# Differential attention: the mix of the two softmaxes on GpSimd alone

## The chip, the cores and the metric

One core of a Trainium2 chip runs the kernel. The metric is the device time of one execution in microseconds. The engines are TensorE (PE in the profile; its weight loads are PEld), VectorE (DVE), ScalarE (ACT), GpSimd (POOL) and SyncE (SP), which issues the DMAs.

## The reference, cut to what matters

Two transformer layers on 2048 tokens of width 1024. The first layer attends in three ways at once: stick-breaking attention (6 heads), differential attention (6 heads), and attention over a memory (4 heads). The change touches the second of these. Each of its heads has two components, each with a softmax of its own over the keys up to the query, and the second softmax is subtracted, with a factor, before the product with the values:

```python
def one_block(bi):
    qi = lax.dynamic_slice_in_dim(q, bi * BLOCK, BLOCK, axis=1)
    s = jnp.einsum('bqhcd,bkhcd->bhcqk', qi, k, ...) * scale
    ...
    p = jax.nn.softmax(jnp.where(causal, s, NEG_BIG), axis=-1)
    a = p[:, :, 0] - lam * p[:, :, 1]
    return jnp.einsum('bhqk,bkhd->bqhd', a.astype(v.dtype), v)
```

An rms norm over each head's 64 features follows, then a gate, the output projection, a layer norm, and the second layer.

## The kernel before, in words

The kernel runs in stages: the projections of the first layer, the stick-breaking attention (to about 1120 us of the span), the differential attention (to about 1740 us), the join of the two layers, and the second layer. Only the differential attention is of concern here; it is the function `differential`.

Its work is cut into 24 units. A unit is a pair of heads (p = 0, 1, 2) and two blocks of 128 queries that together see 17 blocks of keys: a high block of queries with n keys (9 to 16 blocks) and a low block with the rest (8 to 1 blocks). So each row tile is 17 x 128 = 2176 columns wide, with the high block's keys first and the low block's behind them. A unit has four row tiles: x and y, the two components, for each of its two heads.

A unit goes through three stages, each a step behind the one before. While unit s+2 has its scores made, unit s+1 is mixed and unit s multiplied with the values.

- Scores (`diff_scores`): TensorE writes a chunk of up to 512 scores into one of three PSUM banks (`psz`). VectorE moves it to the row tile, negated and scaled, and keeps its minimum (L725), with the mask on the diagonal (L727); L731 joins minima. The bank is free when VectorE is done. ScalarE then takes the exponentials in place, with sums.
- Mix (`diff_mix`): VectorE makes a column of factors per head from the sums: a reciprocal (L762) and a product with minus lambda and the first component's sum (L766). One factor is for the high block and one for the low block. Then x becomes x + factor * y. The softmaxes are not normalised here: the rms norm takes the common factor out.
- Values (`diff_values`): TensorE transposes blocks of x into PSUM (`pstp`), ScalarE copies them to SBUF, and TensorE multiplies with the values. The low block's chunks come first, then the high block's. When four units have filled a chunk of 512 queries, `diff_norm` follows (L849 and L851 are its two GpSimd instructions).

A step has four beats. In a beat the scores of one row tile, the mix's steps for that beat, and chunks of the values are interleaved. Also interleaved is a filler: a share of the output projection (`psmm<-wo,mp`), whose input is split in two parts by ScalarE and GpSimd (L901), and whose result is added up on VectorE (L912).

In this stage the order on TensorE and ScalarE is that in which the program is written. The order on VectorE and GpSimd is chosen by a planner, which simulates the program with its own estimates when it is built. Nine row tiles are there; a unit takes four, y is free again after the mix and x after its transposes.

How the mix is shared before: with nlo the number of the low block's key blocks, `a` is 128 * max(0, 5 - nlo) columns. GpSimd takes columns a to n of a head: it multiplies y by the factor, which is repeated along the row as the second tensor of a two-tensor multiply (L771), and adds the product to x (L772). VectorE takes the low block's columns, in pieces of at most 1024, and columns 0 to a, each as one instruction that multiplies and adds (L778). So VectorE does 5 to 8 of the 17 blocks. Its first piece of a head comes at once with GpSimd's part; the others come a beat or more later.

Of the kernel before, what the change touches and what calls it, by code (L numbers as in the profile page):

```python
# [12 lines left out]
ALU = mybir.AluOpType  # L13
AX = mybir.AxisListType

S = 2048
D = 1024
P = 128
# [16 lines left out]
VBLOCKS = 5  # L35
MIX = 1024
# [9 lines left out]
class Pinned:  # L46
    """An engine whose instructions stay in the order in which they are written."""
# [18 lines left out]
class Net:  # L66
# [15 lines left out]
    @contextmanager  # L82
    def phase(self, bufs, banks, side="left"):
        """Pools for one phase; SBUF slots and PSUM banks by tag."""
        with ExitStack() as ctx:
            layer = {k: (n, ctx.enter_context(self.tc.tile_pool(name=self.nm("p" + k), bufs=1, side=side, reuse_waits="tile")))
                     for k, n in bufs.items()}
            if banks:
                ps = ctx.enter_context(self.tc.tile_pool(name=self.nm("pp"), bufs=1, space=bass.MemoryType.PSUM, reuse_waits="tile"))
                layer.update({"ps" + k: (n, ps) for k, n in banks.items()})  # L90
            self.layers.append(layer)
            yield
            self.layers.remove(layer)
# [20 lines left out]
    def turn(self, key, pattern):  # L114
        """The next letter of a repeated pattern: which engine takes this one."""
        k = self.turns.get(key, 0)
        self.turns[key] = k + 1
        return pattern[k % len(pattern)]
# [8 lines left out]
    def consts(self):  # L127
# [5 lines left out]
        # nothing, then what is after the query (a column further on: at it or after it)  # L133
# [12 lines left out]
        # -lambda on every partition  # L146
# [26 lines left out]
    def rope_tables(self, k, sink):  # L173
        """cos and sin of the positions' angles, in chunks of 512: sink(chunk, cos, sin)."""
        nc = self.nc
        for t in range(NT):
            posi = self.t("c2", I32)
            self.dma(posi, self.i["pos"][t * TC:(t + 1) * TC].partition_broadcast(P))
            ang = self.t("c2")
            nc.vector.tensor_copy(ang, posi)  # L180
            nc.vector.tensor_scalar_mul(ang, ang, self.freq[:, k:k + 1])
            n = self.t("c2")
            nc.vector.tensor_scalar(n, ang, 1.0 / TWO_PI, MAGIC, ALU.mult, ALU.add)
            nc.vector.tensor_scalar_add(n, n, -MAGIC)
            for c in (C1, C2, C3):
                nc.vector.scalar_tensor_tensor(ang, n, -c, ang, ALU.mult, ALU.add)
            nc.vector.tensor_scalar(ang, ang, math.pi, -math.pi, ALU.min, ALU.max)
            nc.scalar.activation(n, ang, AF.Abs)
            sink(t, n, ang)
            yield  # L190

# [1 line left out]
    def wtile(self, src):  # L193
        """A [P, 8, 128] tile of weights, as two parts."""
        w, (fill,) = self.wtile_steps(src, 1, self.nc.gpsimd)
        fill()
        return w
# [21 lines left out]
    def load_x(self, between):  # L219
        """x transposed, [tc][half] -> (hi, lo) of [P, 4, 512]."""  # L220
# [22 lines left out]
    def proj_t(self, w, t):  # L243
        """[128 features, 512 tokens] of chunk t."""
        return self.proj_side([w], t)[0]

    def proj_side(self, ws, t):
        """The same for several tiles of weights side by side."""
# [8 lines left out]
    def spill_parts(self, ps, dst, t, scale=None):  # L257
        """ps (times a power of two) in two parts to dst [2, P, S]."""
# [112 lines left out]
    def rope_all(self):  # L371
        """Both layers' tables to DRAM, a chunk of one at each next()."""
# [13 lines left out]
    def vtile(self, g):  # L386
        """Weights of 256 columns of the two attentions' values, as two parts of each half."""
# [9 lines left out]
    def values(self, g, ws, side):  # L397
        """256 columns of the two attentions' values, token by token."""
# [19 lines left out]
    def dup_parts(self, hi, lo, src, hh):  # L418
        """Half hh of src's partitions, its two parts in both halves of hi and lo."""
# [13 lines left out]
    def memkv(self, W, mem, keep):  # L433
        """Memory keys of each pair of heads and all values, a weight tile at each next()."""
# [35 lines left out]
    def tblocks(self, blocks, pattern="AV"):  # L470
        """Up to four [P, P] blocks transposed, in SBUF."""
# [8 lines left out]
    def softmax_pair(self, z, e, n0, sink=False):  # L480
        """z [P, 2, 256] -> e, normalised; columns from n0 on; the first is the sink's."""
# [13 lines left out]
    def mem_scores(self, qs, qcol, mk):  # L495
        """One block of queries, heads 2f and 2f+1 over the memory."""
# [20 lines left out]
    def load_qstack(self, src, t):  # L517
        """[P = two copies of 64, 2 heads, 2 parts, 512]."""
# [9 lines left out]
    def load_sb(self, p):  # L528
        """A pair of heads' keys and values and the last chunk's queries."""
# [69 lines left out]
    def differential(self):  # L599
        """Differential attention in three stages, each a unit (two blocks of queries, 17 blocks of  # L600
        keys together, of two heads) behind the one before: scores and exponentials; the mix of the
        two softmaxes; the product with the values. Between them go some feature tiles' share of
        the output projection."""
# [10 lines left out]
        def mixed(a, b):  # L614
            """Two lists evenly mixed, each in its order."""
# [58 lines left out]
    def load_dq(self, p, k, h):  # L674
        """Queries of a half of each of the two chunks: units j = 2h and 2h + 1."""
# [7 lines left out]
    def diff_parts(self, unit):  # L683
        """Of the two blocks of queries: their number, the chunk's, the place in it, the keys, the
        first column in a row."""
# [4 lines left out]
    def diff_scores(self, unit, rows):  # L690
        """For each head and component the steps of its scores, and those of the exponentials."""
# [56 lines left out]
    def diff_mix(self, unit, rows):  # L748
        """Steps by beat."""
        p, k, j = unit  # L750
        parts = self.diff_parts(unit)
        nlo = parts[1][3] // P
        a = P * max(0, VBLOCKS - nlo)
        cf = {}

        def take(steps):
            for f in steps:
                f()
# [9 lines left out]
        def mix(hh):  # L768
            x, y = rows[unit][0][2 * hh][0], rows[unit][0][2 * hh + 1][0]
            n = parts[0][3]  # L770
            self.nc.gpsimd.tensor_mul(y[:, a:n], y[:, a:n], cf[hh][:, :1].to_broadcast([P, n - a]))  # L771
            self.nc.gpsimd.tensor_add(x[:, a:n], x[:, a:n], y[:, a:n])  # L772
            pieces = [(c, min(c + MIX, 17 * P), 1) for c in range(n, 17 * P, MIX)]
            if a:
                pieces.append((0, a, 0))
            for lo, hi, w in pieces:
                def piece(lo=lo, hi=hi, w=w):
                    self.nc.vector.scalar_tensor_tensor(x[:, lo:hi], y[:, lo:hi], cf[hh][:, w:w + 1], x[:, lo:hi], ALU.mult, ALU.add)  # L778
                late[hh].append(piece)
            late[hh].pop(0)()  # L780

        late = [], []
        i0, f0, m0, l0 = lambda: inverse(0), lambda: factor(0), lambda: mix(0), lambda: take(late[0])
        i1, f1, m1, l1 = lambda: inverse(1), lambda: factor(1), lambda: mix(1), lambda: take(late[1])
        return [[i0, f0, m0], [l0, i1, f1, m1], [], [l1]]
# [36 lines left out]
    def diff_norm(self, p, t, s0, pv, tail):  # L822
        """rms norm over each head's 64, scaled by the first sum; the rest of its steps to tail."""
# [42 lines left out]
    def filler(self):  # L866
        """alpha x and the share of the output projection of the feature tiles known before the
        differential attention; lists of steps."""
# [60 lines left out]
    def memory(self, mk, mv):  # L929
        """The first layer's attention over the memory, a block at each next(), to go  # L930
        between other projections."""
# [52 lines left out]
    def out_proj(self, w, msrc, spans, res, alpha, lng, lnb, tbs, ahead):  # L984
        """A block of the output projection and its layer norm at each next()."""
# [50 lines left out]
    def join(self, tail):  # L1036
        """The rest of the first layer's output projection, its norm, x of the second layer
        transposed in two parts, and its first gates; the steps in tail go between."""
# [60 lines left out]
    def qstack_head(self, qs, src, hh, eng):  # L1099
        """The two parts of head hh's queries (half of src's partitions), one on top of the other."""  # L1100
# [4 lines left out]
    def qstack_from(self, src, eng):  # L1105
        """[P = two parts of 64, 2 heads, 512] of a tile of two heads' queries (in SBUF)."""
# [22 lines left out]
    def swa_scores(self, qb, head, qs, qcol, ks):  # L1129
        """Heads head and head+1 over a block of keys and the one before; the first  # L1130
        column of that one is out of every query's window and takes the sink."""
# [37 lines left out]
    def gates(self, W, dst, om=None, m1=None, order=None, ws=None):  # L1169
        """silu of the gates to dst; times what has been attended to m1 where that is known."""  # L1170
# [27 lines left out]
    def layer2_kv(self):  # L1198
        """Keys in two parts and values of each group, to DRAM."""
# [35 lines left out]
    def layer2(self):  # L1235
        """The projections of queries go in quarters between the blocks of the attention, whose
        three stages lie a block or two apart."""
# [238 lines left out]
```

## Time and profile before

| | |
|---|---|
| time, median of 3 runs | 2660.3 us (2658.35 to 2661.22) |
| profiled execution, span from the first to the last instruction | 2665.1 us |
| mean granted TensorE clock in it | 0.969 |
| busy in the span: PE, DVE, ACT, POOL | 94%, 62%, 47%, 45% |
| GpSimd's multiply (L771) and add (L772), 48 each | 132.9 and 163.3 us |
| VectorE's multiply-and-add (L778), 72 | 153.2 us |

The profiled execution has no time on record beside its span; the median of the runs is 4.8 us below that span. Durations below are those of the profiled execution. In a row of groups, the columns are the line, engine, operation, output and inputs with their shapes, the count, then busy time and mean duration in ns, then the idle time of the engine just before with what ended it. A row of the timeline begins with the start and the duration in us; brackets hold the idle time before the instruction and what released it. A row of waits gives who waited for whom, the total in us, how often, and the longest.

### The profile page before, as it was taken

How to read it: one execution, taken by the hardware profiler on the slowest of the kernel's cores; microseconds unless marked ns; L12 is line 12 of the kernel's file. 1: busy time of each engine (PE TensorE's matmuls, PEld its weight loads, DVE VectorE, ACT ScalarE, POOL GpSimd, SP SyncE). 2: the span in 40 equal slices, each digit the busy share in tenths (PEclk: the TensorE clock that was granted, in tenths of full speed). 3: DMA queues.
4: the chain of work that ended last, by engine and by line, in shares of the span. 5: the costliest groups of instructions: out<-in, count | busy, mean ns of one | idle time of the engine just before them, and what ended most of it. 6: DMA issues, size and time to landing. Idle time of an engine off the chain costs nothing. (4 is left out here: it accounts for less than half of the span.)

```text
span 2665.1 us, 42634 instructions
## 1 busy us (share of the span) xinstructions
PE 2503.5 (94%) x15564; PEld 1964.7 (74%) x15564; DVE 1656.7 (62%) x3672; ACT 1264.2 (47%) x2653; POOL 1189.9 (45%) x848
## 2 busy tenths in 40 slices
PE   9899999999989999968877988999999999999998
PEld 7788998888757777646655666678788777777887
DVE  5732223421379999888889878788321667677554
ACT  4532222221167777555665765744121677776200
POOL 1301004730056666465646746764541555535333
PEclk9999999999989999989988988999999999999999
DMA  7643223321842331442523422265332555532541
GB/s 273 212 146 125 70 88 105 137 103 52 203 104 70 82 71 34 99 116 73 127 78 95 108 76 74 70 215 173 88 101 75 162 154 162 152 96 99 194 147 67
DMA packets 199250, 311.60 MB, mean 117 GB/s; under 512 B 17921, under 2 KB 97281, under 8 KB 198529
## 3 DMA queue, kind: packets, MB, share of 16 engines
q1 hardware_dynamic: 198464, 307.83, 39.3%
q8 instruction: 123, 2.02, 0.3%
q10 hardware_dynamic: 576, 1.05, 0.1%
q14 instruction: 87, 0.70, 0.1%
HBM read 204.74 MB, written 104.07 MB: 116 GB/s over the span
## 5 line engine op out<-in xcount | busy, mean ns | idle before, releaser
L56 PE MATMUL psmm<-big,w 128*128 128x512 f32 x1680 | 415.4, 395 | 0.0
L56 PEld LDWEIGHTS psmm<-big,w 128*128 128x128 f32 x1680 | 306.8, 189 | 58.3
L586 POOL TENSOR_TENSOR wb<-wb,row 128x512 f32<-128x512 f32 (+3 forms) x192 | 219.5, 1154 | 136.4 <-DVE row L582 126.9
L582 DVE TENSOR_TENSOR_SCAN row<-psz,row,zero 128x512 f32<-128x512 f32 (+5 forms) x240 | 258.5, 1107 | 31.9 <-ACT psz L579 31.6
L253 PE MATMUL psmm<-big,w 128*128 128x512 f32 x1200 | 275.2, 389 | 0.0
L253 PEld LDWEIGHTS psmm<-big,w 128*128 128x128 f32 x1200 | 225.0, 188 | 47.0 <-issue 0.2
L56 ACT ACTIVATE row<-row,mn 128x2048 f32<-128x2048 f32 (+7 forms) x192 | 229.7, 1201 | 33.6 <-DVE mn L731 33.0
L56 PE MATMUL psmm<-big,mp 128*128 128x512 f32 x1056 | 244.5, 392 | 0.0
L725 DVE TENSOR_SCALAR_CACHE_REDUCE row<-psz 128x512 f32<-128x512 f32 (+1 forms) x324 | 200.9, 640 | 58.4 <-PE psz L56 55.9
L56 PEld LDWEIGHTS psmm<-big,mp 128*128 128x128 f32 x1056 | 198.3, 189 | 41.3 <-issue 0.3
L56 ACT COPY wT<-pstp 128x512 f32<-128x512 f32 (+3 forms) x240 | 121.4, 522 | 169.8 <-PE pstp L56 163.0
L1190 DVE TENSOR_TENSOR c<-psmm,c 128x512 f32<-128x512 f32 x62 | 42.6, 691 | 240.3 <-ACT c L1189 240.3
L592 PE MATMUL pspv<-wT,kv 128*64 128x128 f32 x1632 | 158.1, 287 | 15.4 <-ACT wT L122 15.4
L771 POOL TENSOR_TENSOR row<-row,tiny 128x1536 f32<-128x1536 f32 (+3 forms) x48 | 132.9, 2769 | 83.9 <-DVE tiny L766 78.1
L772 POOL TENSOR_TENSOR row<-row,row 128x1536 f32<-128x1536 f32 (+3 forms) x48 | 163.3, 3408 | 1.9
L208 POOL TENSOR_TENSOR w<-w,w 128x1024 fp32r<-128x1024 f32 x20 | 48.8, 2440 | 255.8 <-ACT w L207 155.4
L56 PE MATMUL psmm<-wo,mp 128*128 128x512 f32 x480 | 155.3, 437 | 3.1 <-ACT mp L56 2.3
L578 ACT ACTIVATE wb<-psz 128x512 f32<-128x512 f32 (+3 forms) x240 | 129.9, 541 | 53.6 <-PE pstp L475 37.2
L778 DVE SCALAR_TENSOR_TENSOR row<-row,tiny,row 128x128 f32<-128x128 f32 (+7 forms) x72 | 153.2, 2154 | 0.5
L573 PE MATMUL psz<-kv,qs 128*128 128x512 f32 (+3 forms) x480 | 150.0, 406 | 2.1 <-DVE row L582 2.0
L592 PEld LDWEIGHTS pspv<-wT,kv 128*64 128x64 f32 x1632 | 106.7, 139 | 60.5 <-issue 20.5
L56 PE MATMUL pstp<-ident,row 128*128 128x128 f32 x816 | 142.0, 297 | 9.7 <-DVE c L860 8.1
(222 smaller groups left out, 5241.6 us busy)
## 6 DMA issues: line engine op xcount, KB each, us to landing
silu<-c SPq DMA_DIRECT2D x54, 256.0 KB, 2.3
sl<-silu SPq DMA_DIRECT2D x54, 256.0 KB, 3.3
qs<-sbq SPq DMA_DIRECT2D x48, 256.0 KB, 5.3
cs<-rope SPq DMA_DIRECT2D x24, 512.0 KB, 4.4
kc<-k SPq DMA_DIRECT2D x36, 320.0 KB, 5.1
w<-in_we_dram SPq DMA_DIRECT2D x20, 512.0 KB, 3.7
raw<-in_wo_dram SPq DMA_DIRECT2D x20, 512.0 KB, 4.0
rx<-in_x_dram SPq DMA_DIRECT2D x32, 256.0 KB, 2.7
```

The lines of the kernel that those rows point to most:

```text
L56: return self.tc.keep_in_program_order(f(*a, **k))
L208: eng.tensor_sub(lo[:, sl], raw[:, sl], hi[:, sl].bitcast(F32))
L253: self.nc.tensor.matmul(ps, w[a][:, c, :], self.xpart(t, c, b), start=(c == k == 0), stop=(c == 7 and k == 2))
L573: nc.tensor.matmul(z[:, :m], qs[:, hh, k, qcol], ks[hh][:, lo:hi], start=(k == 0), stop=(k == 1 and not diag))
L578: nc.scalar.activation(w[:, :m], z[:, :m], AF.Sigmoid, scale=0.125)
L582: nc.vector.tensor_tensor_scan(prr[:, lo + s0 - 1:hi - 1][:, ::-1], z[:, s0:m][:, ::-1], self.zero.to_broadcast([P, m - s0]), prr[:, hi - ...
L586: eng.tensor_mul(w[:, :m], w[:, :m], prr[:, lo:hi])
L592: nc.tensor.matmul(pv[64 * hh:64 * hh + 64, qcol], vp[:, blk, 64 * hh:64 * hh + 64], wT[hh][:, j * P:(j + 1) * P], start=(hi == n and j == ...
L725: nc.vector.tensor_scalar(e[:, col + lo:col + lo + n0], z[:, :n0], -scale, before, ALU.mult, ALU.min, accum_out=acc)
L771: self.nc.gpsimd.tensor_mul(y[:, a:n], y[:, a:n], cf[hh][:, :1].to_broadcast([P, n - a]))
L772: self.nc.gpsimd.tensor_add(x[:, a:n], x[:, a:n], y[:, a:n])
L778: self.nc.vector.scalar_tensor_tensor(x[:, lo:hi], y[:, lo:hi], cf[hh][:, w:w + 1], x[:, lo:hi], ALU.mult, ALU.add)
```

## The change

GpSimd does the whole mix, for both blocks of queries. Per head it runs four instructions: for the low block's columns, then for the high block's, a multiply of y by the column of factors and an add to x. The multiply is now a tensor-scalar instruction, which takes the factor as a per-partition scalar instead of as a repeated second tensor. VectorE's pieces, the constants that sized them and the lists that put some of them into later beats are gone. The factors are still made by VectorE. The beats of the two heads' mixes stay the first and the second. Comments and docstrings are removed too.

```diff
-VBLOCKS = 5
-MIX = 1024
...
     def diff_mix(self, unit, rows):
         p, k, j = unit
         parts = self.diff_parts(unit)
-        nlo = parts[1][3] // P
-        a = P * max(0, VBLOCKS - nlo)
         cf = {}
-
-        def take(steps):
-            for f in steps:
-                f()
...
         def mix(hh):
             x, y = rows[unit][0][2 * hh][0], rows[unit][0][2 * hh + 1][0]
             n = parts[0][3]
-            self.nc.gpsimd.tensor_mul(y[:, a:n], y[:, a:n], cf[hh][:, :1].to_broadcast([P, n - a]))
-            self.nc.gpsimd.tensor_add(x[:, a:n], x[:, a:n], y[:, a:n])
-            pieces = [(c, min(c + MIX, 17 * P), 1) for c in range(n, 17 * P, MIX)]
-            if a:
-                pieces.append((0, a, 0))
-            for lo, hi, w in pieces:
-                def piece(lo=lo, hi=hi, w=w):
-                    self.nc.vector.scalar_tensor_tensor(x[:, lo:hi], y[:, lo:hi], cf[hh][:, w:w + 1], x[:, lo:hi], ALU.mult, ALU.add)
-                late[hh].append(piece)
-            late[hh].pop(0)()
-
-        late = [], []
-        i0, f0, m0, l0 = lambda: inverse(0), lambda: factor(0), lambda: mix(0), lambda: take(late[0])
-        i1, f1, m1, l1 = lambda: inverse(1), lambda: factor(1), lambda: mix(1), lambda: take(late[1])
-        return [[i0, f0, m0], [l0, i1, f1, m1], [], [l1]]
+            for w, (lo, hi) in ((1, (n, 17 * P)), (0, (0, n))):
+                self.nc.gpsimd.tensor_scalar_mul(y[:, lo:hi], y[:, lo:hi], cf[hh][:, w:w + 1])
+                self.nc.gpsimd.tensor_add(x[:, lo:hi], x[:, lo:hi], y[:, lo:hi])
+
+        i0, f0, m0 = lambda: inverse(0), lambda: factor(0), lambda: mix(0)
+        i1, f1, m1 = lambda: inverse(1), lambda: factor(1), lambda: mix(1)
+        return [[i0, f0, m0], [i1, f1, m1], [], []]
```

## The prediction

> **What bounds the kernel now.** I read the page first, for the slices, then stretches of the trace: before, during and after the differential attention.
>
> ```profile
> span 2665.1 us, 42634 instructions
> ...
> PE   9899999999989999968877988999999999999998
> ...
> DVE  5732223421379999888889878788321667677554
> ...
> POOL 1301004730056666465646746764541555535333
> PEclk9999999999989999989988988999999999999999
> ```
>
> ```profile
> 1120.00:1734.00 614.00, 514.26 (x3388) 366.39 (x3387) 507.25 (x1393) 379.69 (x681) 370.96 (x146) 0.90 0.36 95
> 1134.80:1730.00 595.20, 496.59 (x3292) 353.41 (x3292) 495.61 (x1346) 370.80 (x668) 369.38 (x145) 0.90 0.34 90
> 1734.00:2665.00 931.00, 904.07 (x5178) 719.68 (x5178) 538.04 (x1399) 404.56 (x970) 424.78 (x313) 0.99 0.44 134
> 0.00:1120.00 1120.00, 1085.20 (x7001) 878.59 (x7002) 611.45 (x882) 480.00 (x1003) 394.13 (x389) 0.99 0.38 115
> ```
>
> The columns of the second view are the stretch, its length, the busy time of PE, PEld, DVE, ACT and POOL, the granted clock, and DMA. Outside the differential stage TensorE is 97% busy; inside, 514.3 of 614 us, at a clock of 0.90. So only this stage, slices 17 to 26, has something to give: about 100 us of idle TensorE, and a little more if the clock comes back. The second row runs from the first multiply of the mix to its last add, for 24 units: 595.2/24 = 24.8 us each, in which PE is busy 20.7, DVE 20.7, ACT 15.5 and POOL 15.4 us.
>
> The waits of the stage say what TensorE lacks:
>
> ```profile
> POOL row L771 <- DVE tiny L766: 78.1, 20, 11.0
> ...
> PE psz L56 <- DVE row L725: 43.2, 27, 9.1
> PE psz L56 <- DVE mn L727: 35.7, 16, 4.9
> ...
> PEld pstp L56 <- POOL row L771: 2.0, 2, 1.0
> ```
>
> 79 us of the 100 are score matmuls waiting for VectorE to empty a score bank. For the mix itself PE waits 2 us: the mixed rows are ready in time. POOL in its turn waits 78 us for the factors, which come from the same late VectorE. VectorE is the bound of the stage, though it is busy only 83% of it.
>
> **What the removed work costs.** These are the stage's groups, then two shapes of one of them, then one moment on POOL, DVE and PE:
>
> ```profile
> L772 POOL TENSOR_TENSOR row<-row,row 128x1536 f32<-128x1536 f32 (+3 forms) x48 | 163.3, 3408 | 1.9
> L778 DVE SCALAR_TENSOR_TENSOR row<-row,tiny,row 128x128 f32<-128x128 f32 (+7 forms) x72 | 153.2, 2154 | 0.5
> L771 POOL TENSOR_TENSOR row<-row,tiny 128x1536 f32<-128x1536 f32 (+3 forms) x48 | 132.9, 2769 | 83.9 <-DVE tiny L766 78.1 <-PE psz L56 5.1
> L901 POOL TENSOR_TENSOR mp<-mp,mp 128x640 fp32r<-128x640 f32 x30 | 50.1, 1670 | 92.5 <-ACT mp L56 68.8 <-PE psmm L56 12.5 <-DMA rp<-rx 11.2
> L766 DVE SCALAR_TENSOR_TENSOR tiny<-s,nlam,tiny 128x2 f32<-128x2 f32 x48 | 26.1, 543 | 0.5
> L849 POOL TENSOR_TENSOR tiny<-tiny,mhalf 128x8 f32<-128x8 f32 x10 | 16.5, 1651 | 62.4 <-DVE tiny L845 62.4
> L851 POOL TENSOR_TENSOR c<-c,tiny 128x512 f32<-128x512 f32 x10 | 10.4, 1044 | 0.0
> ```
>
> ```profile
> L778 DVE SCALAR_TENSOR_TENSOR row<-row,tiny,row 128x128 f32<-128x128 f32 x12 | 26.5, 2208 | 0.0
> L778 DVE SCALAR_TENSOR_TENSOR row<-row,tiny,row 128x1024 f32<-128x1024 f32 x6 | 12.2, 2038 | 0.1
> ```
>
> ```profile
> 1652.39 2.75 POOL L771 TENSOR_TENSOR row<-row,tiny 128x1536 f32<-128x1536 f32 x1
> ```
>
> ```profile
> 1652.44 3.38 DVE L778 SCALAR_TENSOR_TENSOR row<-row,tiny,row 128x640 f32<-128x640 f32 x1
> ```
>
> ```profile
> 1656.50 0.77 PE L56 MATMUL psz<-kc,qa 128*128 128x512 f32 x1 [2.64 <-DVE mn L727]
> ```
>
> L778 takes 2.2 us for 128 columns and 2.0 us for 1024: its length isn't its work. At 1652.44 it begins just behind POOL's multiply, lasts until 0.68 us after that has ended (1655.14), and the score matmul stands for 2.64 us. So VectorE's share of the mix is mostly waiting for GpSimd, and behind it in VectorE's queue stand the bank evacuations. The change takes all 72 away: 153.2 us, 6.4 per unit; DVE falls from 20.7 to 14.3 us per unit. By the Trainium skill, "SBUF — State Buffer", section "Who interferes with whom", a VectorE instruction with two SBUF inputs and a GpSimd instruction that reads SBUF exclude each other for a whole instruction; the 2208 ns of 128 columns agrees.
>
> **What is added on GpSimd.** Per head all 17 blocks, 2176 columns, in two pieces: two multiplies, two adds. Now GpSimd takes 9 to 12 blocks of them. Prices are read where no VectorE instruction of this sort ran beside:
>
> ```profile
> 1338.55 2.75 POOL L771 TENSOR_TENSOR row<-row,tiny 128x1536 f32<-128x1536 f32 x1 [0.43 <-DVE tiny L766]
> 1341.38 3.43 POOL L772 TENSOR_TENSOR row<-row,row 128x1536 f32<-128x1536 f32 x1
> ```
>
> ```profile
> 1530.85 2.65 POOL L772 TENSOR_TENSOR row<-row,row 128x1152 f32<-128x1152 f32 x1
> ```
>
> ```profile
> 1520.23 2.11 POOL L771 TENSOR_TENSOR row<-row,tiny 128x1152 f32<-128x1152 f32 x1 [2.60 <-DVE tiny L766]
> ```
>
> Add: (3.43 - 2.65)/384 = 2.03 ns a column, 0.31 us a piece; 2176 columns in two pieces: 5.04 us. Multiply in its present form (a two-tensor instruction with the factor repeated): (2.75 - 2.11)/384 = 1.67 ns a column and 0.19 us a piece: 4.01 us. But the new multiply is another instruction, a tensor-scalar, which the trace has only on one column:
>
> ```profile
> 1777.32 0.22 POOL L1024 TENSOR_SCALAR tiny<-tiny 128x1 f32<-128x1 f32 x1
> ```
>
> ```profile
> 2506.47 1.31 POOL L1024 TENSOR_SCALAR tiny<-tiny 128x1 f32<-128x1 f32 x1 [1.07 <-DVE tiny L1022]
> ```
>
> ```profile
> 2506.42 1.28 DVE L1026 SCALAR_TENSOR_TENSOR rx<-rx,tiny,gb 128x1024 f32<-128x1024 f32 x1
> ```
>
> Its 1.31 us is again waiting: it ends as VectorE's L1026 does. Free it takes 0.22 us (it adds a constant there, not a column), so its fixed cost is that of L771. Its price per column isn't shown. Lower end: half of L771's, 0.83 ns, since one stream is read and not two. Upper end: POOL's dearest wide instruction:
>
> ```profile
> L208 POOL TENSOR_TENSOR w<-w,w 128x1024 fp32r<-128x1024 f32 x20 | 48.8, 2440 | 255.8 <-ACT w L207 155.4 <-PE psmm L56 100.2
> L278 POOL TENSOR_TENSOR c<-c,w 128x512 f32<-128x512 f32 x24 | 42.3, 1761 | 6.8 <-DVE c L277 6.8
> ```
>
> that is 1761/512 = 3.44 ns, with 2440/1024 = 2.38 between. I take 1.67 ns, L771's, the only row that multiplies a row by a column. The Trainium skill, "GPSIMD Engine Reference", section 4.1 "Engine selection", calls one-input work on GpSimd roughly line-rate; at the 1.2 GHz of its section 1 that is an estimate of 0.83 ns, and the sum would be that of the fast rival below. The same table tells to keep elementwise work on VectorE because GpSimd is about twice slower, which speaks against the change; no run here shows the new multiply.
>
> **The sum.** POOL's mix: 2 x (5.04 + 4.01) = 18.1 us per unit (now 296.2/24 = 12.3). Its other work, L901, L849 and L851, is 77.0/24 = 3.2. Together 21.3, beside PE's 20.7: POOL becomes the longest, by little. What share of the time can a longest engine reach here? The best 26 us of POOL and of PE:
>
> ```profile
> 1276.00:1302.00 26.00, 24.43 (x177) 17.51 (x178) 23.42 (x68) 19.06 (x37) 23.49 (x12) 1.00 0.28 82
> ...
> 1692.00:1718.00 26.00, 24.64 (x191) 17.86 (x189) 21.94 (x76) 18.08 (x33) 19.70 (x10) 1.00 0.24 74
> ```
>
> give 90% (POOL) and 95% (PE). With 92.5% a unit takes 21.3/0.925 = 23.0 us, 1.8 less than now; 24 x 1.8 = 43 us. Latency: a head's mix takes 9.05 us instead of 6.2, but a unit has a whole step for it, and PE waits only 2 us now; the piece needed first, the low block's, is also done first. The last unit ends a few us later, beside transposes and products still queued: nothing. The added instructions issue no DMA; nothing is moved past SP's queue. DVE and POOL are ordered by the planner; TensorE and ScalarE keep their order.
>
> Span 2665.1 - 43 = 2622. The span is 4.8 us above the median of the runs, 2660.3, so **2617** on that scale.
>
> **Rivals.**
> (a) *GpSimd's multiply is cheap* (0.83 ns): 2 x (5.04 + 2.19) + 3.2 = 17.7 us, PE is the bound: 20.7/0.95 = 21.8, 72 us gained: 2588. If the clock rises from 0.90 to 0.95 as well, PE needs 19.7 and the gain is 98: 2562. For it: one stream. Against: GpSimd's rows all cost 1.67 ns or more.
> (b) *GpSimd becomes the bound above the present period.* Place: the mix that the transposes of the next step stand behind. At 2.38 ns the unit has 2 x (5.04 + 5.56) + 3.2 = 24.4 us, /0.925 = 26.4: 38 us lost, 2698; at 3.44 ns 29.0, 31.4 and 158 lost, 2818. It decides from 22.9 us of POOL per unit, that is from 2.05 ns a column, just above what the add costs. For it: most of POOL's rows lie between 2.0 and 2.4, and only the repeated-factor form below. Against: the multiply with a column is that form's work.
> (c) *The block moves to L766.* The factor instruction also reads two small SBUF tensors, and most of its mean of 543 ns is waiting, as two of them show:
>
> ```profile
> 1651.13 1.19 DVE L766 SCALAR_TENSOR_TENSOR tiny<-s,nlam,tiny 128x2 f32<-128x2 f32 x1
> ...
> 1662.63 0.22 DVE L766 SCALAR_TENSOR_TENSOR tiny<-s,nlam,tiny 128x2 f32<-128x2 f32 x1
> ```
>
>  With POOL 90% busy in instructions of 9.05/4 = 2.3 us, it waits for about half of one or more, some 1.3 us, 2.7 per unit; evacuations and the next mix stand behind it. If TensorE pays all of that, 20.7 + 2.7 = 23.4, /0.95 = 24.6: no change, 2656. Against: three score banks, and DVE then has 8 us free per unit.
>
> **Chances.** Forecast, 2590 to 2645: 0.41. (a) 0.13. (b) 0.39. (c) 0.07. A measurement of this kernel can tell 0.2%, 5 us, from no change. Faster 0.54, same 0.07, slower 0.39. The range, **2565 to 2720**, leaves out the far end of (b), above 2.7 ns, and the last of (a). The forecast's own range is 2590 to 2645.
>
> **What would show it.** Right: no mix on DVE; score matmuls wait for DVE well under 79 us; POOL 85 to 95% busy in the stage; tensor-scalar on 1536 columns near 2.75 us; clock above 0.90; everything before 1120 unchanged. Wrong: a tensor-scalar above 3.3 us on 1536 columns, with transposes waiting for POOL (b); L766 above 1.2 us with PE still waiting for banks (c); tensor-scalar near 1.5 us and POOL with gaps (a).

## The result, and the profile after

The changed kernel takes 2683.7 us (median of 4 runs, 2683.3 to 2687.6) against 2660.0 us for the kernel before (4 runs). The ratio is 1.0095, with a 95% interval from 1.0081 to 1.0109: it is slower, by 24 us or 0.95%. The forecast was 2617 us. The time lies inside the stated range, but on the side of rival (b).

From the page of the changed kernel, the span, the busy times, and the slices:

```profile
span 2682.1 us, 42712 instructions
...
PE 2497.1 (93%) x15564; PEld 1962.5 (73%) x15564; DVE 1573.9 (59%) x3600; ACT 1264.5 (47%) x2653; POOL 1417.9 (53%) x944
...
PE   9899999999889999879788788789999999999998
...
POOL 1301005730156666489999999975541555534333
```

In slices 19 to 26, counted from 1, GpSimd is now at nine tenths or more, and TensorE's holes are still there. The stretch from the first multiply of the mix to its last add gives the sum (columns: stretch, length, busy PE, PEld, DVE, ACT, POOL, granted clock, DMA share, GB/s):

```profile
1133.00:1751.50 618.50, 499.31 (x3357) 357.14 (x3357) 416.25 (x1279) 375.26 (x676) 599.45 (x243) 0.89 0.35 93
```

It is 618.5 us long, 25.8 us per unit, where it was 595.2 and 24.8. That is 23 us longer, as much as the loss of 24 between the medians. The two profiled spans differ by 17 us only, since the one before lay above its median and is 6 us longer outside the stage. GpSimd is busy 599.5 of them, 97%. VectorE fell from 496 to 416 us, and this brought no gain here. The groups of the stage and two shapes of the new multiply:

```profile
L764 POOL TENSOR_SCALAR row<-row,tiny 128x128 f32<-128x128 f32 (+7 forms) x96 | 289.1, 3026 | 10.2 <-DVE tiny L758 5.2 <-DVE mn L725 2.1 <-ACT wT L54 2.1
L765 POOL TENSOR_TENSOR row<-row,row 128x128 f32<-128x128 f32 (+7 forms) x96 | 240.7, 2530 | 0.0
```

```profile
L764 POOL TENSOR_SCALAR row<-row,tiny 128x2048 f32<-128x2048 f32 x6 | 32.7, 5449 | 0.0
...
L764 POOL TENSOR_SCALAR row<-row,tiny 128x128 f32<-128x128 f32 x6 | 3.7, 612 | 6.6 <-DVE tiny L758 2.4 <-DVE mn L725 2.1 <-ACT wT L54 2.1
```

The tensor-scalar costs (5449 - 612)/1920 = 2.52 ns a column, and 0.29 us besides. The sum had 1.67 and 0.19. The six multiplies of each width agree within 0.04 us (5.44 to 5.46 us for 2048 columns), so this is the instruction's own price and not a wait. It is dearer than the add, though it reads one row and not two. The waits of the stage show what became of it:

```profile
PEld pstp L54 <- POOL row L765: 76.3, 23, 7.5
PE pstp L54 <- POOL row L765: 68.7, 18, 7.3
...
PE psz L54 <- DVE row L723: 29.7, 18, 8.7
...
PE psz L54 <- DVE mn L725: 3.3, 4, 1.7
```

TensorE's waits for score banks fell from 79 to 33 us, as forecast. In their place it waits 69 us for GpSimd's adds, which it did not do before. These waits, and the 4.16 us of a multiply on 1536 columns, are the signs that the prediction had named for rival (b).

### The profile page after: what moved, and what is told of

It reads as the page before. It is cut to its first block, busy times and chain, and to the rows that moved or that the text cites. A ratio compares the mean times of both kernels' runs of the same rounds, so it can differ in the third digit from the quotient of the medians.

```text
span 2682.1 us, 42712 instructions
## 1 busy us (share of the span) xinstructions
PE 2497.1 (93%) x15564; PEld 1962.5 (73%) x15564; DVE 1573.9 (59%) x3600; ACT 1264.5 (47%) x2653; POOL 1417.9 (53%) x944
## 3 DMA queue, kind: packets, MB, share of 16 engines
q8 instruction: 124, 2.03, 0.3%
## 5 line engine op out<-in xcount | busy, mean ns | idle before, releaser
L764 POOL TENSOR_SCALAR row<-row,tiny 128x128 f32<-128x128 f32 (+7 forms) x96 | 289.1, 3026 | 10.2 <-DVE tiny L758 5.2
L723 DVE TENSOR_SCALAR_CACHE_REDUCE row<-psz 128x512 f32<-128x512 f32 (+1 forms) x324 | 202.0, 642 | 84.9 <-PE psz L54 81.8
L765 POOL TENSOR_TENSOR row<-row,row 128x128 f32<-128x128 f32 (+7 forms) x96 | 240.7, 2530 | 0.0
L54 PEld LDWEIGHTS pstp<-ident,row 128*128 128x128 f32 x816 | 102.7, 151 | 105.1 <-POOL row L765 76.3
```

Source lines behind the costliest of these rows:

```text
L54: return self.tc.keep_in_program_order(f(*a, **k))
L723: nc.vector.tensor_scalar(e[:, col + lo:col + lo + n0], z[:, :n0], -scale, before, ALU.mult, ALU.min, accum_out=acc)
L764: self.nc.gpsimd.tensor_scalar_mul(y[:, lo:hi], y[:, lo:hi], cf[hh][:, w:w + 1])
L765: self.nc.gpsimd.tensor_add(x[:, lo:hi], x[:, lo:hi], y[:, lo:hi])
```

## The experiments

Theory A: GpSimd's sum of work is the bound, because the new multiply costs 2.52 ns a column. Rival B: the planner's order on GpSimd (two to four multiplies ahead of their adds) makes the rows late. Rival C: the factor instruction, stuck behind GpSimd, holds the score banks. Line numbers shift a little between kernels. Every ratio is to the kernel before, run on the same chip.

### The multiply put back to a repeated factor

```diff
-                self.nc.gpsimd.tensor_scalar_mul(y[:, lo:hi], y[:, lo:hi], cf[hh][:, w:w + 1])
+                self.nc.gpsimd.tensor_mul(y[:, lo:hi], y[:, lo:hi], cf[hh][:, w:w + 1].to_broadcast([P, hi - lo]))
```

> The changed kernel with one thing put back: GpSimd multiplies with the factor repeated along the row as a second tensor, in the changed kernel's pieces. Theory A (GpSimd's work is the bound, because the tensor-scalar multiply costs 2.52 ns a column where 1.67 was forecast): GpSimd's multiplies fall from 289.1 us to 48 x 4.01 = 192 us, 4.0 us per unit, so GpSimd needs 21.2 us per unit; the period falls from 25.8 to about 21.8, where TensorE (20.7/0.95) stands, and the time to about 2684 - 96 = 2588 us. Rival B (the order is at fault: the planner puts both multiplies of a head ahead of its adds, so the rows come late whatever the sum): the order stays, TensorE still waits for the last adds, and the time stays above 2640 us. Rival C (the factor instruction stuck behind GpSimd holds VectorE, and with it the score banks): its waits stay, so 2630 to 2660 us.

Measured: 2601.5 us, ratio 0.9789 (0.9774 to 0.9803). The stretch of the mix and its groups:

```profile
1135.00:1672.00 537.00, 480.44 (x3341) 343.99 (x3340) 404.46 (x1273) 372.26 (x673) 498.79 (x242) 0.94 0.39 105
```

```profile
L765 POOL TENSOR_TENSOR row<-row,row 128x128 f32<-128x128 f32 (+7 forms) x96 | 239.7, 2527 | 0.0
L764 POOL TENSOR_TENSOR row<-row,tiny 128x128 f32<-128x128 f32 (+7 forms) x96 | 190.5, 2010 | 16.7 <-DVE tiny L758 11.8 <-PE psmm L54 3.2 <-PE pstp L54 0.9
```

This one line is worth 82 us. The planner's order changed with it, but not as rival B would have it: counted in the traces, four multiplies stand in a row ahead of their adds 18 times here, and 11 times in the changed kernel. Multiplies take 190.5 us (forecast: 48 x 4.01 = 192), GpSimd 499 us in all, and the stage 537. So the move of the work to GpSimd does gain 57 us; the instruction chosen for the multiply turned it into a loss of 24. The expectation's 2588 was 13 us too low: GpSimd is busy 93% of this stage, and the expectation had let its share rise to that of the changed kernel.

### The same instruction in the kernel before

```diff
-            self.nc.gpsimd.tensor_mul(y[:, a:n], y[:, a:n], cf[hh][:, :1].to_broadcast([P, n - a]))
+            self.nc.gpsimd.tensor_scalar_mul(y[:, a:n], y[:, a:n], cf[hh][:, :1])
```

> The kernel before with GpSimd's multiply as a tensor-scalar instruction, the shares of the two engines unchanged. Theory A: GpSimd needs 48 x (0.29 + 2.52 x 1.44 - 0.19 - 1.67 x 1.44) / 24 = 2.6 us more per unit, 18.0 of 24.8, and is not the bound: no change, 2655 to 2668 us. The reading that VectorE's pieces wait for whole GpSimd instructions adds to it: those that begin behind a multiply (25 of 72) wait 1.2 us longer, 30 us in all on VectorE, which is the bound here: 2670 to 2690 us.

Measured: 2639.5 us, ratio 0.9931 (0.9916 to 0.9946). Both expectations missed: a dearer multiply made this kernel faster. Its groups:

```profile
L771 POOL TENSOR_SCALAR row<-row,tiny 128x1536 f32<-128x1536 f32 (+3 forms) x48 | 197.8, 4121 | 69.2 <-DVE tiny L766 49.1 <-ACT wT L56 6.8 <-DVE mn L731 6.5
...
L778 DVE SCALAR_TENSOR_TENSOR row<-row,tiny,row 128x128 f32<-128x128 f32 (+7 forms) x72 | 130.7, 1840 | 0.6
```

GpSimd's multiplies grew by 65 us and VectorE's pieces shrank by 22. One moment in each kernel shows a way in which they shrink. In the kernel before, on GpSimd and on VectorE:

```profile
1352.12 2.75 POOL L771 TENSOR_TENSOR row<-row,tiny 128x1536 f32<-128x1536 f32 x1 [7.31 <-DVE tiny L766]
1354.94 3.43 POOL L772 TENSOR_TENSOR row<-row,row 128x1536 f32<-128x1536 f32 x1
```

```profile
1353.20 5.72 DVE L778 SCALAR_TENSOR_TENSOR row<-row,tiny,row 128x128 f32<-128x128 f32 x2
```

Two pieces (128 and 512 columns) take 5.72 us: they end at 1358.9, half a microsecond after the add. With the tensor-scalar:

```profile
1327.03 4.16 POOL L771 TENSOR_SCALAR row<-row,tiny 128x1536 f32<-128x1536 f32 x1
1331.28 3.48 POOL L772 TENSOR_TENSOR row<-row,row 128x1536 f32<-128x1536 f32 x1
```

```profile
1327.46 3.66 DVE L778 SCALAR_TENSOR_TENSOR row<-row,tiny,row 128x128 f32<-128x128 f32 x2
```

Both pieces are over at 1331.1, ahead of the end of the multiply (1331.2). The repeated-factor multiply keeps VectorE out until it ends, and the add then comes at once and keeps the second piece out too. The tensor-scalar lets VectorE in before it ends; here both pieces end in its last microsecond. Counted over both traces, 47 of the 72 pieces meet one tensor-scalar and nothing else of GpSimd's: 33 of them end in its last 0.75 us, 13 more than three microseconds before its end, and one behind it. In the kernel before, the largest group, 21, spans a multiply and the add behind it, and no piece ends in the last 0.75 us of a multiply. The planner's order changed as well, so how much of the 19 us is from each isn't settled.

### VectorE's pieces left out

```diff
-            for lo, hi, w in pieces:
...
-                late[hh].append(piece)
-            late[hh].pop(0)()
```

> The kernel before without VectorE's pieces of the mix; the low block's columns and the first columns of some high blocks stay unmixed, so this part of the computation is left out. It shows what relief VectorE gets from the removal alone, with GpSimd at its old 15.4 us per unit. Theory A: VectorE was the bound; without 6.4 us per unit it needs 14.3, TensorE becomes the bound at 20.7/0.95 = 21.8 us per unit, 2588 us, and less if the clock comes back. Rival B: the banks would be late anyway because the score matmuls come in bursts: 2640 us or more.

Measured: 2555.3 us, ratio 0.9622 (0.9606 to 0.9638). The mix's stretch:

```profile
1132.00:1613.00 481.00, 453.23 (x3279) 326.57 (x3278) 358.25 (x1277) 367.70 (x666) 351.52 (x145) 0.97 0.42 110
```

VectorE was the bound: without its pieces the time falls by 103 us (the stage by 114, measured from a profiled execution that lay above the median), and TensorE is busy 94% of the stage. TensorE itself needs only 453 us where 497 were counted, mostly because its clock is 0.97 and not 0.90: 496.6 x 0.90/0.97 = 461. The expectation (2588) had left the clock out, and only its "less if the clock comes back" covers the rest.

### Less of the mix on VectorE

```diff
-VBLOCKS = 5
+VBLOCKS = 0
```

In the kernel before, this gives VectorE's second piece to GpSimd, in the repeated-factor form.

> The kernel before with VectorE's second piece (the first columns of the high block, where the low block has under five blocks) given to GpSimd in its repeated-factor form; VectorE keeps the low block. The reading that a VectorE piece waits for whole GpSimd instructions: 24 of 72 pieces go, some 2.3 us each, 55 us of VectorE, while GpSimd rises from 15.4 to about 16.6 us per unit: 2615 to 2645 us. The rival, that VectorE pays by column: 60 blocks of 276 go, at most a fifth of 153 us, and the time moves by less than 12 us: 2648 to 2665 us.

Measured: 2601.5 us, ratio 0.9790 (0.9776 to 0.9805). The groups:

```profile
L772 POOL TENSOR_TENSOR row<-row,row 128x2048 f32<-128x2048 f32 (+7 forms) x48 | 178.6, 3727 | 1.6
L771 POOL TENSOR_TENSOR row<-row,tiny 128x2048 f32<-128x2048 f32 (+7 forms) x48 | 146.7, 3057 | 39.3 <-DVE tiny L766 32.6 <-ACT wT L56 3.2 <-PE psmm L56 2.2
L778 DVE SCALAR_TENSOR_TENSOR row<-row,tiny,row 128x128 f32<-128x128 f32 (+7 forms) x48 | 91.7, 1910 | 0.6
```

VectorE's pieces cost by the piece and not by the column: a third of the pieces went, with 22% of the columns (60 of 276 blocks), and 40% of the time went with them (153.2 to 91.7 us). The kernel gained 57 us, more than the 13 to 43 expected, and as much as with all of the mix on GpSimd in the cheap form.

### Factors that do not wait

```diff
-            self.nc.vector.scalar_tensor_tensor(cf[hh], self.dsum[p, k][:, i0:i1 + 1:i1 - i0], self.nlam, cf[hh], ALU.mult, ALU.mult)
+            for w, i in enumerate((i0, i1)):
+                self.nc.vector.tensor_scalar(cf[hh][:, w:w + 1], self.dsum[p, k][:, i:i + 1], self.nlam, cf[hh][:, w:w + 1], ALU.mult, ALU.mult)
```

> The changed kernel with the factors made by two one-column tensor-scalar instructions on VectorE per head, which read one tensor and two scalar columns, instead of one instruction that reads two tensors. Theory A: GpSimd stays the bound with 25.2 us per unit: 2680 to 2688 us, whatever the factor instruction does. Rival C: the factor instructions (58.2 us, of which about 48 are waits of up to 9.3 us behind GpSimd) held the banks; without the waits 2635 to 2660 us. If the one-input form waits as well, the factor lines still show means above 0.8 us and the run says nothing about C.

Measured: 2713.7 us, ratio 1.0212 (1.0197 to 1.0227): slower still. The factors, the waits, and the stretch:

```profile
L759 DVE TENSOR_SCALAR tiny<-s,nlam,tiny 128x1 f32<-128x1 f32 x96 | 22.0, 268 | 0.7
```

```profile
PEld pstp L54 <- POOL row L766: 120.4, 20, 15.3
PE pstp L54 <- POOL row L766: 114.1, 18, 15.0
```

```profile
1132.00:1776.00 644.00, 492.95 (x3326) 352.38 (x3324) 379.01 (x1326) 373.59 (x673) 599.74 (x242) 0.86 0.33 89
```

The factors no longer wait (22.0 us where 58.2 went), and there is no gain, so C does not explain the loss. GpSimd's work is the same 600 us, and the stage is 25 us longer, all of it GpSimd's idle time: 44 us and not 19. So the sum is a floor, and A alone does not say how far above it the stage lies. Most of the added idle time stands before the norm's first GpSimd instruction, here and then in the changed kernel:

```profile
POOL tiny L834 <- DVE tiny L830: 22.6, 8, 7.1
```

```profile
POOL tiny L833 <- DVE tiny L829: 6.9, 9, 2.3
```

The planner had changed the order on VectorE and GpSimd as well; the next runs ask what the order does.

### The mix near its written order

```diff
+            pool = Pinned(self.nc.gpsimd, self.tc)
...
-                self.nc.gpsimd.tensor_scalar_mul(y[:, lo:hi], y[:, lo:hi], cf[hh][:, w:w + 1])
-                self.nc.gpsimd.tensor_add(x[:, lo:hi], x[:, lo:hi], y[:, lo:hi])
+                pool.tensor_scalar_mul(y[:, lo:hi], y[:, lo:hi], cf[hh][:, w:w + 1])
+                pool.tensor_add(x[:, lo:hi], x[:, lo:hi], y[:, lo:hi])
```

Pieces of the next head still slip between a multiply and its add, but no row of multiplies goes ahead of a whole mix.

> The changed kernel with GpSimd's mix instructions held near the order in which they are written: a piece's add comes soon after its multiply, and no head's multiplies go ahead of the whole mix of the head before. In the changed kernel the planner puts two to four multiplies in a row ahead of their adds. Theory A (GpSimd's sum): its work stays 25.2 us per unit, 605 us for 24, and it was busy 599 of 618.5 us, so no more than 2% of the stage can be won: 2672 to 2688 us. Rival B (the order): TensorE's 69 us of waiting for adds mostly go, 2625 to 2655 us. If the run before it (factor with one input, 2714 us at the same GpSimd sum) was slow by its order, this one should stand at A's lower end, 2670 to 2678.

Measured: 2731.4 us, ratio 1.0265 (1.0241 to 1.029), the slowest of all. The stretch, and what GpSimd waited for:

```profile
1151.50:1798.50 647.00, 499.05 (x3347) 355.28 (x3348) 394.60 (x1260) 371.96 (x671) 600.05 (x244) 0.87 0.32 86
```

```profile
POOL mp L886 <- ACT mp L54: 38.6, 11, 12.4
POOL mp L886 <- PE psz L54: 20.5, 3, 12.6
POOL tiny L834 <- DVE tiny L830: 10.8, 5, 4.8
```

Rival B is not borne out: with an order close to the written one TensorE waits 121 us for the adds, and not 69. GpSimd's work is again 600 us. Its first multiply comes at 1151.5 and not at 1133.0, behind two of the filler's splits (L886) that stand 12.6 and 12.4 us before they can begin, and it stands idle for 47 us after that. What the three orders share is that GpSimd stands in its queue before something that isn't ready. Which instructions ahead of which cost how much was not taken apart. The order is worth tens of microseconds, then, but neither it nor the factors' waits can be the loss: the changed kernel's GpSimd is idle for only 19 us of its stage, and without any idle time it would still take about 2684 - 19 = 2665 us, an estimate, against 2660 before.

The same order with the repeated factor:

> The repeated-factor kernel (2601 us) with the mix held near its written order in the same way. There GpSimd was busy 499 of 537 us. Theory A: 499 is the floor of its stage, at most 30 us to win if the order lets GpSimd work without gaps: 2575 to 2598 us. Rival B: TensorE's waits for adds there were only 9 us, so the order has at most that to give: 2592 to 2603 us.

Measured: 2619.8 us, ratio 0.9846 (0.9819 to 0.9872): 18 us behind the kernel with the planner's order, against both expectations. Beside the run before it, it shows the price of the instruction with the mix in nearly one order: 2731.4 against 2619.8, 112 us.

The repeated factor with the factors that do not wait:

> The repeated-factor kernel with the one-input factors, which do not wait behind GpSimd. Its multiplies again go ahead in rows of two to four, more so than in the repeated-factor kernel. Rival C (the factor's waits, 53 us there, hold the score banks): 2570 to 2588 us. Rival B (the order of multiplies ahead of adds costs, as in the one-input run): 2600 to 2625 us.

Measured: 2602.4 us, ratio 0.9787 (0.9772 to 0.9802): the same as without (2601.5). TensorE's waits for L723 fell from 24.4 to 6.3 us, and those for GpSimd's adds rose from 9.2 to 29.5. The time lies in rival B's range, but not by its mechanism: four multiplies stand in a row only 6 times here, against 18 in the kernel without. What TensorE no longer waits for at a score bank, it waits for at a mixed row tile; why was not taken apart. With the factors in this form in both, the dearer multiply costs 111 us (2713.7 against 2602.4).

Both together:

> The repeated-factor kernel with both: mix near its written order, and one-input factors. If the waits for banks (31 us of TensorE) come from the factors, and the order costs nothing any more, the stage comes down to GpSimd's 499 us: 2565 to 2580 us. If neither counts, 2592 to 2603 us as with the order alone.

Measured: 2603.2 us, ratio 0.9794 (0.9776 to 0.9812). This is the expectation's second case: the two together gain nothing over the planner's order alone. With the order held, though, the factors are worth 17 us (2619.8 to 2603.2).

### Less work on GpSimd: ScalarE multiplies the low block

```diff
...
+        def low(hh):
+            x, y = rows[unit][0][2 * hh][0], rows[unit][0][2 * hh + 1][0]
+            n = parts[0][3]
+            self.nc.scalar.mul(y[:, n:], y[:, n:], cf[hh][:, 1:2])
+            self.nc.gpsimd.tensor_add(x[:, n:], x[:, n:], y[:, n:])
...
+        return [[i0, f0, m0], [l0, i1, f1, m1], [l1], []]
```

GpSimd keeps the high block with the repeated factor, and all adds.

> The repeated-factor kernel (2601 us) with the low block's multiply on ScalarE, a beat later, and its add on GpSimd. Theory A (GpSimd's sum is still the floor there: 499 of 537 us): a low block has 4.5 blocks on average, so GpSimd loses 48 x (0.19 + 1.67 x 0.576) = 55 us, the stage falls towards TensorE's and 480 to 500 us, 2565 to 2585 us. Rival: ScalarE, whose order is fixed, stands at each multiply until the factor is there, and TensorE's copies stand behind it: 2600 to 2630 us.

Measured: 2583.2 us, ratio 0.9719 (0.9702 to 0.9735), within theory A's range. With the factors that do not wait:

> The same with the factors made by two one-input instructions on VectorE, which do not wait behind GpSimd. If ScalarE stands at the factors, this is faster than the run with the low block on ScalarE alone, by up to 20 us; if GpSimd's sum or TensorE is the floor, the two agree within 5 us.

Measured: 2575.1 us, ratio 0.9686 (0.9671 to 0.9700): the fastest complete kernel, 83 us (3.1%) under the kernel before and 109 us under the changed one. Its groups and its stretch:

```profile
L764 POOL TENSOR_TENSOR row<-row,tiny 128x2048 f32<-128x2048 f32 (+7 forms) x48 | 137.5, 2867 | 9.8 <-DVE tiny L759 9.8
...
L54 ACT ACTIVATE row<-row,tiny 128x128 f32<-128x128 f32 (+7 forms) x48 | 37.3, 777 | 0.0
```

```profile
1135.00:1642.00 507.00, 465.05 (x3325) 335.29 (x3323) 359.18 (x1322) 398.21 (x719) 446.48 (x193) 0.96 0.40 108
```

53 us of GpSimd's multiplies became 37 us on ScalarE, which is busy for 398 of the 507 us. GpSimd is down to 88% and TensorE up to 92% of the stage. The factors that do not wait, worth nothing with the planner's order in the kernel that this one comes from, are worth 8 us here.

## Why the prediction was wrong

**The bound of the kernel before: right.** VectorE held the score banks, and its pieces of the mix were mostly waiting. Leaving the pieces out gains 103 us; giving away only the second piece gains 57. The gain named as the most there could be, 98 us with the clock back, is near.

**The price of the add and GpSimd's other work: right.** 5.04 us per head were forecast for the add, 240.7/48 = 5.01 came. What else GpSimd does stayed, 3.1 us per unit where 3.2 were counted. Latency, put at nothing, holds only near the forecast's own price: TensorE waits 9 us for the adds with the repeated factor, and 69 with the tensor-scalar.

**The price of the multiply: the step that failed.** The prediction took 1.67 ns a column, "the only row that multiplies a row by a column", for an instruction that the trace had only on one column. It is 2.52: 6.0 us per head and not 4.01, 4.0 us per unit in all, and past the 2.05 ns from which rival (b) decides. Put back to the priced form, the same change gives 2601.5 us, inside the forecast's own range of 2590 to 2645. There GpSimd needs 498.8/24 = 20.8 us per unit (forecast 21.3) and is busy 93% of the stage (forecast 92.5%). So the mechanism was right, and one term was mis-sized. By the prediction's own working, 22.9 us per unit were enough to undo the gain that 21.3 gave, and so that term set the sign.

The Trainium skill, "GPSIMD Engine Reference", section 4.1 "Engine selection", has one-input work on GpSimd at roughly line-rate. The trace does not agree: 2.52 ns a column, three times the 0.83 ns estimated from it, and more than the two-row add's 2.03. The measurement decides. The same section's rule that VectorE is the place for elementwise work does not hold for this kernel either: the mix on GpSimd with a repeated factor is 57 us faster, for here the two engines wait for each other. VectorE's pieces took 2154 ns on average and 341 at the least, and GpSimd's multiplies and adds 296.2 us beside them, 281.8 without them.

**The share that the longest engine can reach: too low.** 92.5% was taken; at the new price GpSimd reached 97% (599.5 of 618.5). At 92.5%, its real 599.5/24 = 25.0 us per unit would have made 27.0 and a loss of 53 us, not 24. The two errors ran against each other: price too low, share too low.

**Rival (c): half right.** The factor's mean rose to 1.2 us, close to the 1.3 of waiting that was said. But taking its waits away won nothing in the changed kernel: that run is 30 us slower, with the order changed too.

**Chances.** (b) had 0.39 and the forecast 0.41. Its price range (2.38 to 3.44 ns) held the truth; its times (2698 to 2818) were too long, by the share. The choice between them rested on a row of another instruction, and that row said nothing on the new one's rate.

## What to carry to other kernels

A new instruction's rate need not be that of the instruction it replaces, even where the arithmetic is the same and fewer operands are read; where the sum lies within a few per cent of what would undo the gain, that one price decides the sign, so put it into the chances and measure it first. Read a mean duration beside its smallest and beside its size: pieces that take as long for 128 columns as for 1024 are waiting, and then the number of pieces matters, not their width. When an engine is nearly full, waits that are removed elsewhere can come back as waits for it; in these runs, taking work off it was what paid.

## What the runs showed of the hardware that was not expected

A tensor-scalar on GpSimd costs more per column (2.52 ns) than an add of two rows (2.03) or a multiply with a factor repeated along the row (1.67). But it lets VectorE's two-input instructions in before it ends, where the repeated-factor multiply holds them to its end. A piece of 128 columns ends 0.73 us before the tensor-scalar, one of 640 columns 0.20; with the shortest times of these sizes in the kernel before, 0.34 and 0.89 us, both began about 1.1 us before its end, an estimate. With the slower GpSimd instruction the kernel before became faster, 2639.5 us against 2658.4; what part of this the planner's changed order has isn't known.

A small VectorE instruction that reads two tensors can wait through several GpSimd instructions in a row, not only the one that runs. In the changed kernel, four adds and a factor of two columns:

```profile
1512.06 9.79 POOL L765 TENSOR_TENSOR row<-row,row 128x896 f32<-128x896 f32 x4
```

```profile
1512.58 9.29 DVE L758 SCALAR_TENSOR_TENSOR tiny<-s,nlam,tiny 128x2 f32<-128x2 f32 x1
```

The factor ends with the last of the four. This is the longest of 48; the median factor takes 0.24 us. The Trainium skill, "SBUF — State Buffer", section "SBUF: two separate sides", has whichever of the two instructions starts first hold the shared pair of ports for its whole length, with the other blocked. The trace agrees for the repeated-factor multiply and not for the tensor-scalar, which lets VectorE in about 1.1 us before its end. The factor that stands through four adds waits longer than the one instruction that was running when it came.
